# Second feed-forward products: 8 or 9 of 16 units by Strassen's scheme instead of 7, with one to three weight sums of a unit made in DRAM

## The chip, the cores and the metric

The kernel runs on one core of a Trainium2 chip. The metric is the device time of one execution in microseconds (us), lower is better. Before the change it is 1324.59 us, the median of 3 runs (1323.66 to 1324.63).

## What is computed

A trunk of four layers works on 256 tokens of width 1024 in float32. Each layer adds a token mixer and then a feed-forward block to the residual stream; the mixers are retention (layers 0 and 3), a convolution module (layer 1) and stick-breaking attention (layer 2). A last RMS norm follows. The change is in the feed-forward block:

```
def squared_relu_mlp(xn, w1, w2):          # w1: 1024 x 4096, w2: 4096 x 1024
    h = jax.nn.relu(xn @ w1)
    return (h * h) @ w2

for i in range(DEPTH):                     # DEPTH = 4
    x = x + mixer(rms_norm(x, norm_mix[i]))
    x = x + squared_relu_mlp(rms_norm(x, norm_ffn[i]), ffn_w1[i], ffn_w2[i])
```

## The kernel before

**Numbers.** Every float32 operand of a large product is split into a rounded part (`hi`, type fp32r) and the rest (`lo`); a product is three matmuls, hi·hi, hi·lo and lo·hi (`triple`, L721, one 128x512 matmul each). For a weight, ACT copies `hi` (L367) and DVE subtracts to get `lo` (L374).

**Weights.** All weights are packed on the host into 220 chunks of 128 x 2048 floats (1 MB), in the order in which they are used. One chunk holds two units of 1024 columns. SP loads chunks with plain DMAs (L349) into three buffers `raw`; the units' hi and lo lie in five buffers each (`wh`, `wl`). SP issues its DMAs strictly in its own order, and so do POOL, DVE, ACT and PE with their instructions: an instruction that waits for a semaphore holds back all that stand behind it on its engine. A scheduler orders the instructions of each engine; in the stick-breaking mixer PE and ACT keep the order in which the code was written.

**Second feed-forward product** (`down`). The 4096 inner columns are 16 units `kb` of 256. The result has four 128x512 blocks C[t, c] (two token halves t, two column halves c) in PSUM. A plain unit is eight block products, 24 matmuls. A unit of the list `FAST` uses Strassen's scheme in Winograd's form: seven block products, 21 matmuls. With A the unit's 2 x 2 activation blocks and B its weight blocks, the seven products take A11, A12, A22 and the sums S1 = A21 - A22, S2 = A11 - S1, S3 = A11 - A21, S4 = A12 - S2 on one side, and B11, B21, B22 and T1 = B11 + B12, T2 = T1 + B22, T3 = B12 + B22, T4 = T2 + B21 on the other (`fast_unit`). T1, T2 and T4 are added by DVE (L415, L417, L419). T3 is made in a temporary by two transfers: SP loads B12 (L385), then POOL issues a transfer that accumulates B22 onto it (L386); the tile is fetched two fast units ahead (`sum_ahead`). The S sums are made by DVE in the stage before, as each inner column group comes out of the first product (L680 to L682), and are split at L684 (ACT) and L685 (DVE). Before the change seven of 16 units are fast in each layer; 13 units (`MIXED`) come first, fast and plain in turn, and three plain ones (`REST`) last.

**POOL elsewhere.** POOL also adds squares for the norms (L519, and L527 in `norm_r`), adds halves of the retention's q and k squares (L968), writes the convolution's strips, and in stick-breaking attention clears one tile for each of the four head groups b (L1637). ACT then writes a masked copy of q into this tile (L1640), and PE reads it (L1662) together with the image of k that ACT makes next (L1633).

Of the kernel before, what the change touches and what calls it, by code (L numbers as in the profile page):

```python
# [15 lines left out]
P = 128  # L16
# [42 lines left out]
FAST = (5, 6, 9, 12, 13, 14, 15)  # L59
MIXED = (0, 1, 5, 2, 6, 3, 9, 12, 4, 13, 14, 7, 15)  # L60
REST = (8, 10, 11)
# [7 lines left out]
def _plan():  # L69
    u = []  # L70
    for i in range(DEPTH):
# [30 lines left out]
        u += [("ffn_w2", i, "a", kb, c * 512) for kb in MIXED for c in range(2)]  # L102
        u += [("ffn_w2", i, "a", kb, c * 512) for c in range(2) for kb in REST]
# [6 lines left out]
NCHUNK = NUNIT // UPC  # L110
DECAY = [PLAN.index(u) // UPC + n for u in (PLAN[DST * UPC], ("ret_w_in", 1, "b", 0, DK)) for n in range(RH)]


def _pack_weights(inp):
    out = np.empty((NCHUNK, P, UPC * 1024), np.float32)
    for n, (name, l, kind, kb, c0) in enumerate(PLAN):
# [3 lines left out]
        if kind == "qk":  # L120
            blk = np.concatenate([blk[:, c0 : c0 + 256], blk[:, D + c0 : D + c0 + 256]], axis=1)
        else:
            blk = blk[:, c0 : c0 + nc_]
        o = out[n // UPC, :, (n % UPC) * 1024 : (n % UPC + 1) * 1024]
# [119 lines left out]
class Trunk:  # L244
    def __init__(self, ctx, tc, xT, w, prm, cst, fin, gn, out):
# [18 lines left out]
        self.sums, self.later = [], []  # L264
# [72 lines left out]
    def unit_hi(self, key):  # L337
# [3 lines left out]
        if o == 0:  # L341
# [3 lines left out]
            else:  # L345
                self.rawt = self.raw.tile([P, RAWW], F32, name=self.nm("raw"), tag="raw")
                h = 1024 if n < 4 else UPC * 1024
                for a in range(0, UPC * 1024, h):
                    nc.sync.dma_start(self.rawt[:, a : a + h], self.w_d[n][:, a : a + h])  # L349
# [27 lines left out]

    def sum_ahead(self, l):
        nc = self.nc
        m = len(self.ahead)  # L380
        if m < len(FAST):
            kb = [k for k in MIXED if k in FAST][m]
            d = self.w_d[PLAN.index(("ffn_w2", l, "a", kb, 0)) // UPC]
            t = self.tmp()
            nc.sync.dma_start(t, d[:, 1024:1536])  # L385
            self.tc.keep_in_program_order(nc.gpsimd.dma_start(t, d[:, 1536:2048], accum_op=ALU.add))  # L386
            self.ahead[kb] = t


    def fast_unit(self, name, l, kb):  # L390
# [13 lines left out]
        with self.tc.issue_after(self.lo_ins):  # L404
            hi, lo = self.unit((name, l, "a", kb, 0))
        out = [(hi[:, c : c + 512], lo[:, c : c + 512]) for c in (0, 512)]
        o = self.un % UPC * 1024
        assert PLAN[self.un] == (name, l, "a", kb, 512) and o
        self.un += 1
        b11, b21, t1, b22 = (self.rawt[:, i * 512 : (i + 1) * 512] for i in range(4))  # L410
        t3 = self.ahead[kb]
        self.sum_ahead(l)
        t2, t4 = (self.tmp() for _ in range(2))
        with self.tc.issue_after(self.lo_ins):
            nc.vector.tensor_add(t1, b11, t1)  # L415
        parts(self.rawt[:, 1024:2048])
        nc.vector.tensor_add(t2, t1, b22)  # L417
# [3 lines left out]
        out[2], out[3] = out[3], out[2]  # L421
        return out
# [99 lines left out]
    def norm_r(self, halves=True):  # L522
        nc = self.nc
        sq, n = self.sq, 2
        if halves:
            sq, n = sq[:, :S], 1
            nc.gpsimd.tensor_add(sq, sq, self.sq[:, S:])  # L527
# [122 lines left out]
    def ffn(self, i, nxt):  # L650
        nc = self.nc
        last = nxt is None
        h, rb, fast, room = [], [], {}, []

        def spare(n):
            if n < 4:
                return self.bigt(F32R)
            if n < 6:
                if n == 4:
                    room.append(self.cp.tile([P, RH * 384], F32R, name=self.nm("room"), tag="decay"))  # L660
                return room[0][:, (n - 4) * 512 : (n - 3) * 512]
            return self.zp.tile([P, 512], F32R, name=self.nm("z"), tag=f"z{n - 6}")

        def act(ps):
# [9 lines left out]
            p = len(h) // 2  # L674
            how = "dve" if p < 4 else "act"
            h.extend((self.split(s[:, :S], how), self.split(s[:, S:], how)))
            if p in FAST:
                x = self.tmp()
                s3, s1, s2, s4 = (x[:, n * P : (n + 1) * P] for n in range(4))
                nc.vector.tensor_sub(v3(x[:, :S], 2, P), v3(s[:, :S], 2, P), v3(s, 2, S)[:, :, P:])  # L680
# [1115 lines left out]
```

## Time and profile before

| | us |
|---|---|
| median of 3 runs | 1324.59 |
| the profiled execution | 1323.18 |
| its span, first to last instruction | 1321.4 |
| PE busy in the span | 1311.8 (99%) |
| DVE busy | 1090.9 (83%) |
| ACT busy | 869.7 (66%) |
| POOL busy | 185.3 (14%) |

The profile is of one execution, 1.4 us shorter than the median; 1.8 us of it lie outside the span. The four second feed-forward products stand at 293 to 377, 567 to 651, 858 to 942 and 1231 to 1315 us of the span, stick-breaking attention at about 651 to 757, the second retention at about 942 to 1125. A matmul's busy time overlaps the next one's, so the distance between starts, not the mean of one, tells PE's pace.

### The profile page before, as it was taken

The numbers are of one execution on the slowest core, as the hardware profiler recorded it, in microseconds if no ns is written. First come the engines' busy times: TensorE is split into PE (matmuls) and PEld (weight loads), VectorE is DVE, ScalarE is ACT, GpSimd is POOL, SyncE is SP. The second block draws the span as 40 slices with busy tenths as digits, with TensorE's granted clock in tenths as the row PEclk, the third lists the DMA queues.
The fourth block names the chain that finished last, engine by engine and source line by source line (L and its number), as shares of the span: only waits on it lengthen the run. The fifth ranks groups of instructions, "written<-read, shape, count | busy, mean of one in ns | idle before, by whom it ended". The sixth has DMA issues, their size and how long they took to land.

```text
span 1321.4 us, 20394 instructions
## 1 busy us (share of the span) xinstructions
PE 1311.8 (99%) x7679; PEld 1129.8 (86%) x7679; DVE 1090.9 (83%) x1845; ACT 869.7 (66%) x1419; POOL 185.3 (14%) x197
## 2 busy tenths in 40 slices
PE   9999999999999999999999999999999999999998
PEld 8988888888899898888888898888888888888886
DVE  7988877888988688789878588889898776799896
ACT  7555546885666478866768678856665554567664
POOL 3654411001009120010000010010120000100100
PEclk9999999999999999999999999999999999999999
DMA  8566655558785645587443355586554554555773
GB/s 313 206 219 231 228 207 190 193 190 264 234 304 153 207 178 194 189 245 247 170 183 128 128 194 190 190 269 227 219 185 174 190 180 158 201 204 182 243 237 114
DMA packets 54690, 269.43 MB, mean 204 GB/s; under 512 B 6336, under 2 KB 11584, under 8 KB 27200
## 3 DMA queue, kind: packets, MB, share of 16 engines
q1 hardware_dynamic: 47968, 253.45, 54.4%
q0 software_dynamic: 5760, 12.06, 4.4%
q10 hardware_dynamic: 864, 2.62, 0.6%
q8 instruction: 60, 0.98, 0.3%
q14 instruction: 38, 0.31, 0.1%
HBM read 261.46 MB, written 6.65 MB: 203 GB/s over the span
## 4 chain that ended last, share of the span: by engine, by line
PE 97%; DVE 1%; ACT 1%; POOL 0%; issue 0%; POOLq 0%; ACTq 0%
PE acc L604 22%; PE acc L721 19%; PE acc L600 11%; PE acc L1145 6%; PE acc L1147 6%; PE acc L1146 6%; PE mis L721 6%; PE acc L584 3%; PE acc L585 3%; PE acc L586 3%; PE mis L604 2%; PE acc L1313 1%; PE mis L600 1%; PE acc L1446 1%; PE mis L464 1%; PE mis L1034 1%
## 5 line engine op out<-in xcount | busy, mean ns | idle before, releaser
L374 DVE TENSOR_TENSOR wl<-raw,wh 128x1024 fp32r<-128x1024 f32 (+1 forms) x412 | 505.0, 1236 | 110.3 <-ACT wh L367 107.4
L367 ACT CAST wh<-raw 128x1024 fp32r<-128x1024 f32 (+1 forms) x412 | 423.9, 1041 | 198.3 <-PE acc L1147 67.2
L604 PE MATMUL acc<-z,wh 128*128 128x512 f32 x1152 | 399.4, 393 | 0.0
L600 PE MATMUL acc<-z,wl 128*128 128x256 f32 x1152 | 317.6, 280 | 0.0
L604 PEld LDWEIGHTS acc<-z,wh 128*128 128x128 f32 x1152 | 214.2, 187 | 47.1
L721 PE MATMUL acc<-wh,big 128*128 128x512 f32 x704 | 228.7, 391 | 0.0
L600 PEld LDWEIGHTS acc<-z,wl 128*128 128x128 f32 x1152 | 216.9, 189 | 2.4 <-DVE t L629 0.3
L721 PEld LDWEIGHTS acc<-wh,big 128*128 128x128 f32 x704 | 132.2, 188 | 27.1
L1145 PE MATMUL acc<-wh,z 128*128 128x512 f32 x352 | 138.6, 394 | 0.0
L1147 PE MATMUL acc<-wh,z 128*128 128x512 f32 x352 | 137.3, 390 | 0.0
L1146 PE MATMUL acc<-wl,z 128*128 128x512 f32 x352 | 137.2, 390 | 0.0
L721 PE MATMUL acc<-wl,big 128*128 128x512 f32 x352 | 137.0, 389 | 0.0
L386 POOL DMA_DIRECT2D t<-in_w x28 | 24.9, 1089 | 458.5 <-DMA t<-in_w 327.5
L628 ACT COPY t<-acc 128x256 f32<-128x256 f32 x154 | 53.2, 372 | 47.1 <-PE acc L604 45.5
L1145 PEld LDWEIGHTS acc<-wh,z 128*128 128x128 f32 x352 | 66.1, 188 | 15.2 <-issue 2.2
L1147 PEld LDWEIGHTS acc<-wh,z 128*128 128x128 f32 x352 | 66.1, 188 | 14.9 <-issue 0.8
L721 PEld LDWEIGHTS acc<-wl,big 128*128 128x128 f32 x352 | 66.1, 188 | 13.4
L1146 PEld LDWEIGHTS acc<-wl,z 128*128 128x128 f32 x352 | 66.1, 188 | 13.3
L519 POOL TENSOR_TENSOR t<-t,t 128x512 f32<-128x512 f32 x15 | 24.2, 1613 | 340.8 <-ACT t L514 310.5
L629 DVE TENSOR_TENSOR t<-acc,t 128x256 f32<-128x256 f32 x154 | 59.5, 419 | 13.6 <-ACT t L628 12.6
L399 ACT CAST wh<-raw 128x1024 fp32r<-128x1024 f32 x28 | 29.5, 1052 | 58.5 <-DVE raw L415 56.2
L584 PE MATMUL acc<-z,wh 128*128 128x256 f32 x224 | 63.7, 284 | 0.0
(312 smaller groups left out, 2314.3 us busy)
## 6 DMA issues: line engine op xcount, KB each, us to landing
raw<-in_w SPq DMA_DIRECT2D x214, 1024.0 KB, 4.9
t<-in_w SPq DMA_DIRECT2D x28, 256.0 KB, 5.5
t<-in_w POOLq DMA_DIRECT2D x28, 256.0 KB, 6.0
strip<-st POOLq DMA_DIRECT2D x36, 128.0 KB, 3.8
big<-strip SPq DMA_DIRECT2D x18, 256.0 KB, 5.9
big<-in_gn SPq DMA_DIRECT2D x16, 256.0 KB, 5.3
raw<-in_w SPq DMA_DIRECT2D x7, 512.0 KB, 7.8
raw<-hd SPq DMA_DIRECT2D x8, 263.0 KB, 5.5
```

What stands on the lines that cost most here:

```text
L367: nc.scalar.copy(hi[:, s], src[:, s])
L374: self.lo_ins = self.nc.vector.tensor_sub(lo[:, s], src[:, s], hi[:, s]).ins
L584: nc.tensor.matmul(o, wh[:, kk, cs], ah, start=st, stop=False, **kw)
L585: nc.tensor.matmul(o, wh[:, kk, cs], al, start=False, stop=False, **kw)
L600: mm = nc.tensor.matmul(ps[m][:, :S], wl[:, kk, cs], a[:, :S], start=first and kk == 0, stop=False, **kw)
L604: nc.tensor.matmul(ps[m], wh[:, kk, cs], a, start=False, stop=last and kk == 3, **kw)
L628: nc.scalar.copy(o[:, s], ps[m][:, S:])
L629: nc.vector.tensor_add(o[:, s], ps[m][:, :S], o[:, s])
L721: mm = nc.tensor.matmul(o, l, r, start=start and n == 0, stop=stop and n == 2, skip_group_check=True)
L1145: nc.tensor.matmul(ps[t], zh[:, s], wh[:, kk], start=k == 0, stop=False, skip_group_check=True)
L1146: nc.tensor.matmul(ps[t], zh[:, s], wl[:, kk], start=False, stop=False, skip_group_check=True)
L1147: nc.tensor.matmul(ps[t], zl[:, s], wh[:, kk], start=False, stop=k == 7, skip_group_check=True)
```

## The change

Layers 0 and 1 get eight fast units and layers 2 and 3 nine, so 34 instead of 28. The packed order of a fast unit becomes B21, B11, B22, B12. A new table `AHEAD` names, for each layer, chunks of earlier stages and a number m from 1 to 3: when that chunk is loaded, `make_sums` makes the first m of T1, T3 and T2 for one fast unit in a DRAM tile. SP copies B12 into it once or twice, POOL issues an accumulating transfer of B11 (and B22) onto that, and for m = 3 POOL copies T1 and accumulates B22 onto the copy. Layer 0 has seven such units with m = 2, layer 1 six with m = 1, layers 2 and 3 nine with m = 3. When the fast unit itself is loaded, SP takes 1536 columns from the weights, T1 from the DRAM tile in place of B12, and T3 and T2 into temporaries. What was not made ahead is made as before. On the activation side S1 is written over A21 and split with the rest of the activations, so three sums of 128 columns are split apart and not four. `norm_r` in the second retention adds on DVE and no longer on POOL.

```diff
-FAST = (5, 6, 9, 12, 13, 14, 15)
-MIXED = (0, 1, 5, 2, 6, 3, 9, 12, 4, 13, 14, 7, 15)
-REST = (8, 10, 11)
+FAST = 2 * [(3, 5, 7, 9, 12, 13, 14, 15)] + 2 * [(3, 5, 7, 9, 11, 12, 13, 14, 15)]
+MIXED = 2 * [(0, 1, 3, 5, 2, 7, 9, 4, 12, 13, 6, 14, 15)] + 2 * [(0, 1, 3, 5, 2, 7, 9, 11, 4, 12, 13, 14, 15)]
+REST = 2 * [(8, 10, 11)] + 2 * [(6, 8, 10)]
+AHEAD = {
...
+    2: [(n, 3) for n in (110, 112, 114, 116, 118, 121, 129, 133, 137)],
+    3: [(n, 3) for n in (163, 166, 169, 172, 175, 178, 181, 184, 196)],
+}
...
+                made = self.made.get((key[1], key[3])) if key[2] == "f" else None
+                if made:
+                    h = 1536
+                for a in range(0, UPC * 1024 // h * h, h):
                     nc.sync.dma_start(self.rawt[:, a : a + h], self.w_d[n][:, a : a + h])
+                if made:
+                    d, m = made
+                    nc.sync.dma_start(self.rawt[:, h : h + 512], d[:, :512])
+                    self.fetched = [self.tmp() for _ in range(m - 1)]
+                    for a, t in enumerate(self.fetched):
+                        nc.sync.dma_start(t, d[:, 512 * (a + 1) : 512 * (a + 2)])
...
+            if self.un // UPC in JOBS:
+                self.make_sums(*JOBS[self.un // UPC])
...
+    def make_sums(self, l, kb, m):
+        nc = self.nc
+        w = self.w_d[CHUNK[l, kb]]
+        d = self.dram.tile([P, m * 512], F32, name=self.nm("sums"), tag=f"sums{l}_{kb}", bufs=1)
+        n = min(m, 2)
+        src = w[:, 1536:2048].unsqueeze(1).to_broadcast([P, n, 512])
+        self.tc.keep_in_program_order(nc.sync.dma_start(v3(d[:, : n * 512], n, 512), src))
+        nc.gpsimd.dma_start(d[:, : n * 512], w[:, 512 : 512 + n * 512], accum_op=ALU.add)
+        if m == 3:
+            nc.gpsimd.dma_start(d[:, 1024:], d[:, :512])
+            nc.gpsimd.dma_start(d[:, 1024:], w[:, 1024:1536], accum_op=ALU.add)
+        self.made[l, kb] = d, m
...
-            nc.gpsimd.tensor_add(sq, sq, self.sq[:, S:])
+            (nc.vector if halves == "dve" else nc.gpsimd).tensor_add(sq, sq, self.sq[:, S:])
...
+                s3, s2, s4 = (x[:, n * P : (n + 1) * P] for n in range(3))
+                nc.vector.tensor_sub(s3, a11, a21)
+                nc.vector.tensor_sub(a21, a21, a22)
+                nc.vector.tensor_sub(s2, a11, a21)
+                nc.vector.tensor_sub(s4, a12, s2)
...
-                    self.norm_r()
+                    self.norm_r("dve" if j else True)
```

Three places show how the instructions move. Line numbers after the change are higher (L1637 becomes L1697, L374 becomes L395, L400 becomes L432, L419 becomes L459).

POOL before, from the end of layer 1's second product on: the last two accumulating transfers, the four cleared tiles of stick-breaking attention, the next norm's first add.

```order
L386 DMA t_1371_6840<-in_w 128x512
L386 DMA t_1388_6923<-in_w 128x512
L1637 MEMSET big_7500 128x512
L1637 MEMSET big_7675 128x512
L1637 MEMSET big_7856 128x512
L1637 MEMSET big_8031 128x512
L519 TENSOR_TENSOR t_1749_8448<-t_1745_8413,t_1748_8446 128x512
```

POOL after, inside stick-breaking attention: `sums` are the DRAM tiles of the jobs at chunks 112, 114, 116 and 118; DMAHW is the landing of a transfer that SP issued, DMASW of one that POOL issued.

```order
L408 DMA sums_7542<-sums_7542 128x512 [waits DMASW7_49,DMASW5_49]
L1697 MEMSET big_7604 128x512 [waits PE_49]
L408 DMA sums_7688<-sums_7688 128x512 [waits DMASW6_49,DMASW0_49]
L409 DMA sums_7542<-in_w 128x512 [waits DMASW7_49,DMASW1_49]
L409 DMA sums_7688<-in_w 128x512 [waits DMASW0_49]
L406 DMA sums_7868<-in_w 128x1024 [waits DMAHW4_49]
L408 DMA sums_7868<-sums_7868 128x512 [waits DMASW4_49,DMASW3_49]
L1697 MEMSET big_7784 128x512 [waits PE_49]
L409 DMA sums_7868<-in_w 128x512 [waits DMASW4_49]
L406 DMA sums_8060<-in_w 128x1024 [waits DMAHW7_49]
L408 DMA sums_8060<-sums_8060 128x512 [waits DMASW6_49]
L1697 MEMSET big_7970 128x512 [waits DVE_49]
```

The four tiles were cleared one after the other before; now the tiles of b = 0, 1 and 2 each stand behind an L406 and an L408 of a job, and these wait for landings.

DVE before, one fast unit of the last layer (kb 12): the first half's lo, T1, T2, T4, and the lo of the second half, T3, T2 and T4.

```order
L374 TENSOR_TENSOR wl_13554<-raw_13551,wh_13553 128x1024
L415 TENSOR_TENSOR raw_13551<-raw_13551 128x512
L417 TENSOR_TENSOR t_2858_13560<-raw_13551 128x512
L419 TENSOR_TENSOR t_2859_13561<-t_2858_13560,raw_13551 128x512
L400 TENSOR_TENSOR wl_13564<-raw_13551,wh_13563 128x1024
L400 TENSOR_TENSOR wl_13569<-t_2828_13425,wh_13568 128x512
L400 TENSOR_TENSOR wl_13569<-t_2858_13560,wh_13568 128x512
L400 TENSOR_TENSOR wl_13576<-t_2859_13561,wh_13575 128x512
```

DVE after, the fast unit kb 13 of the last layer (`raw_13941`) between parts of its neighbours.

```order
L459 TENSOR_TENSOR t_2984_14004<-t_2979_13993,raw_13989 128x512
L432 TENSOR_TENSOR wl_13917<-t_2960_13908,wh_13916 128x512
L395 TENSOR_TENSOR wl_13949<-raw_13941,wh_13948 128x1024
L432 TENSOR_TENSOR wl_13953<-raw_13941,wh_13952 128x1024
L459 TENSOR_TENSOR t_2996_14052<-t_2991_14041,raw_14037 128x512
L432 TENSOR_TENSOR wl_13958<-t_2966_13944,wh_13957 128x512
L432 TENSOR_TENSOR wl_13958<-t_2967_13945,wh_13957 128x512
L432 TENSOR_TENSOR wl_13965<-t_2972_13956,wh_13964 128x512
```

The adds of T1 and T2 are gone where m = 3, and the add of T4 (L459) now stands a unit or more ahead of its use.

POOL before, in the second retention's first head: the halves of q's squares, the add of `norm_r`, and the halves of k's and of the next heads'.

```order
L968 TENSOR_TENSOR big_10329<-t_2147_10324 128x256
L527 TENSOR_TENSOR t_2146_10322<-t_2146_10322 128x256
L968 TENSOR_TENSOR big_10329<-t_2167_10406 128x256
L968 TENSOR_TENSOR big_10475<-t_2181_10470 128x256
L968 TENSOR_TENSOR big_10475<-t_2195_10534 128x256
```

DVE after, at the same place: `norm_r`'s add is L566.

```order
L558 TENSOR_TENSOR t_2208_10507<-t_2206_10503,t_2207_10505 128x512
L395 TENSOR_TENSOR wl_10679<-raw_10671,wh_10678 128x1024
L1036 TENSOR_TENSOR t_2218_10535<-t_2210_10511,cst 128x512
L1037 TENSOR_TENSOR t_2219_10536<-t_2210_10511,cst 128x512
L566 TENSOR_TENSOR t_2208_10507<-t_2208_10507 128x256
```

The add left POOL's queue for DVE's, three instructions behind the sum that it reads.

More of the change, by code (lines that the diff above doesn't have):

```diff
@@ L263, in __init__ @@
         self.rest = self.end = None
-        self.sums, self.later = [], []
+        self.sums, self.later, self.made = [], [], {}
         nc = self.nc
@@ L375, in unit_lo @@
         return hi, lo
+    def make_sums(self, l, kb, m):
[10 more added lines that the diff above has]
+        self.made[l, kb] = d, m
     def sum_ahead(self, l):
         nc = self.nc
[L380 to L387, printed above, removed]
+        kbs = [kb for kb in FAST[l] if kb not in self.ahead and self.made.get((l, kb), (0, 0))[1] < 2]
+        if kbs:
+            w, t = self.w_d[CHUNK[l, kbs[0]]], self.tmp()
+            nc.sync.dma_start(t, w[:, 1536:2048])
+            self.tc.keep_in_program_order(nc.gpsimd.dma_start(t, w[:, 1024:1536], accum_op=ALU.add))
+            self.ahead[kbs[0]] = t
     def fast_unit(self, name, l, kb):
@@ L420, in fast_unit @@
         parts(t4)
-        out[2], out[3] = out[3], out[2]
-        return out
+        return [out[i] for i in (1, 0, 2, 3, 4, 5, 6)]
     def unit_raw(self, key, tag, eng=None):
@@ L732, in down @@
         C = {}
+        quick, mixed, late_kb = FAST[i], MIXED[i], REST[i]
         self.ahead = {}
```

115 lines of the change are left out of this document (71 added, 44 removed).

## The prediction

> **What bounds the kernel now.** I began with the page's busy times and its chain of waits, then asked who PE waited for, and then for the four stages of the second product.
>
> ```profile
> span 1321.4 us, 20394 instructions
> PE 1311.8 (99%) x7679; PEld 1129.8 (86%) x7679; DVE 1090.9 (83%) x1845; ACT 869.7 (66%) x1419; POOL 185.3 (14%) x197
> ...
> PE 97%; DVE 1%; ACT 1%; POOL 0%; issue 0%; POOLq 0%; ACTq 0%
> ```
>
> PE is busy for 99% of the span, and the chain that ends last lies on it for 97%. Nothing else bounds the whole. Its waits for others are few:
>
> ```profile
> PE mis L301 <- POOL t L273: 1.3, 1, 1.3
> PE mis L464 <- POOL t L527: 0.7, 1, 0.7
> ```
>
> So the time falls only where PE has fewer columns to stream, or where one of these waits goes; it rises wherever PE is made to wait. The stage that the change shortens, seen alone (only the matmuls of L721; columns: stretch, its length, PE busy and count, granted clock, DMA share, GB/s):
>
> ```profile
> 293.00:377.00 84.00, 82.78 (x363) 1.00 0.83 273
> 567.00:651.00 84.00, 82.76 (x363) 1.00 0.76 244
> 858.00:942.00 84.00, 82.75 (x363) 1.00 0.76 249
> 1231.00:1315.00 84.00, 82.81 (x363) 1.00 0.63 201
> ```
>
> The four stages take the same time for the same 363 matmuls, 82.75 / 363 = 0.228 us each, at full clock: PE never starves there, whatever DMA and DVE do.
>
> **Part by part.**
>
> *Fewer matmuls.* A unit that becomes fast drops one block product, three matmuls. Six more units are fast (34 against 28): 18 x 0.228 = 4.1 us less. The built order has 18 PE rows fewer, so this part does happen. It counts in full only if the operands still come in time.
>
> *DVE and ACT in the second product.* The rows of DVE by shape in the third of these stages (count | busy, mean ns | idle before):
>
> ```profile
> L374 DVE TENSOR_TENSOR wl<-raw,wh 128x1024 fp32r<-128x1024 f32 x24 | 28.8, 1222 | 3.1 <-ACT wh L367 2.7
> L400 DVE TENSOR_TENSOR wl<-t,wh 128x512 fp32r<-128x512 f32 x21 | 13.3, 686 | 3.2 <-ACT wh L399 3.2
> L419 DVE TENSOR_TENSOR t<-t,raw 128x512 f32<-128x512 f32 x7 | 4.9, 693 | 0.2
> L417 DVE TENSOR_TENSOR t<-raw 128x512 f32<-128x512 f32 x7 | 4.8, 692 | 0.2
> L415 DVE TENSOR_TENSOR raw<-raw 128x512 f32<-128x512 f32 x7 | 4.8, 686 | 0.0
> ```
>
> A fast unit costs DVE two lo's of 1024 columns, three of 512 and three adds: 2 x 1.22 + 6 x 0.69 = 6.6 us, against 21 x 0.228 = 4.8 us on PE. A plain unit costs DVE 2.4 and PE 24 x 0.228 = 5.5 us. With m = 3 two adds go: 5.2 us. Over layer 2 or 3 that is 14 adds less (9.7 us) and two more units at 5.2 - 2.4 = 2.8 us: DVE ends 4 us lighter, although four fast units in a row leave it 4 x 0.4 = 1.6 us behind, which the plain unit before them (3.1 us to spare) covers. Layers 0 and 1 keep two or three adds and take one more unit, which comes out within 1 us of before, with at most two fast units in a row. I cost it at nothing; without that cover it would be some 1 us a stage. On ACT a fast unit keeps its 3584 columns of hi. The sums S cost DVE four small subtractions instead of three and a lo of 384 columns instead of 512, in the first product, where they lie beside matmuls: nothing.
>
> *Transfers in the second product.* T3's accumulation goes for 27 of 34 units (layer 1 keeps all eight, layer 0 one); 768 KB of weights and one to three loads of 256 KB come instead. For m = 3 the unit moves 1.5 MB, as before (1 MB, 256 KB and an accumulation of 256 KB). SP's loads of T3 and T2 wait for a temporary, and the next chunk stands behind them. In the stage above ACT already waited for T3's accumulation without PE noticing:
>
> ```profile
> L399 ACT CAST wh<-t 128x512 fp32r<-128x512 f32 x21 | 11.7, 617 | 5.6 <-DMA t<-in_w 4.4 <-PE acc L721 1.2
> ```
>
> So 4 us late in a stage stays hidden, and I cost this at nothing.
>
> *The wait that goes.* PE's 0.7 us at L464 ends with POOL's add of `norm_r`:
>
> ```profile
> 959.95 0.38 PE L464 MATMUL mis<-cst,t 128*128 128x1 f32 x2 [0.68 <-POOL t L527]
> ...
> 953.77 4.81 POOL L968 TENSOR_TENSOR big<-t 128x256 f32<-128x256 f32 x1 [56.81 <-ACT t L959]
> 958.54 1.35 POOL L527 TENSOR_TENSOR t<-t 128x256 f32<-128x256 f32 x1
> ...
> 953.81 0.69 DVE L519 TENSOR_TENSOR t<-t,t 128x512 f32<-128x512 f32 x1
> ```
>
> What it reads is ready on DVE at 953.81 + 0.69 = 954.5, but POOL is held by the add before it. On DVE the add comes after one lo and two products (1.22 + 2 x 0.69 us), about 957, and PE asks at 959.95 - 0.68 = 959.3: the 0.7 us goes, and nothing is late next. At worst it stays.
>
> *The jobs: transfers into DRAM.* Each adds one SP issue behind a chunk's load and one to three POOL instructions. The loads queued behind it come a little later, which ACT's casts don't feel, since they wait for PE to free their buffers and not for DMA:
>
> ```profile
> L367 ACT CAST wh<-raw 128x1024 fp32r<-128x1024 f32 (+1 forms) x412 | 423.9, 1041 | 198.3 <-PE acc L1147 67.2
> ```
>
> What PE can feel is POOL's queue. In stick-breaking attention the clearing of ACT's tile now waits behind an accumulation's landing (the order above). ACT keeps its written order there, so its masked copy of q holds everything behind it: k's image, the casts, the exponentials; PE waits for k's image. The price, from the loads of chunks 116 (for b = 1), 117 and 118 (for b = 2):
>
> ```profile
> 680.55 0.33 SPq L349 DMA_DIRECT2D raw<-in_w  x1
> ...
> 688.63 0.33 SPq L349 DMA_DIRECT2D raw<-in_w  x1
> ...
> 696.37 0.33 SPq L349 DMA_DIRECT2D raw<-in_w  x1
> ...
> 691.49 0.94 ACT L1640 ACTIVATE big<-mis,prm 64x256 f32<-64x256 f32 x2
> 692.45 0.69 ACT L1633 ACTIVATE big<-mis,prm 128x512 f32<-128x512 f32 x1
> ...
> 694.32 1.06 PE L1662 MATMUL mis<-big,big 128*128 128x128 f32 x8
> ...
> 707.78 0.94 ACT L1640 ACTIVATE big<-mis,prm 64x256 f32<-64x256 f32 x2
> 708.75 0.69 ACT L1633 ACTIVATE big<-mis,prm 128x512 f32<-128x512 f32 x1
> ...
> 711.28 0.94 PE L1662 MATMUL mis<-big,big 128*128 128x128 f32 x7
> ```
>
> For b = 1 ACT needs the tile 691.49 - 680.55 = 10.9 us after the load's issue, and PE has 694.32 - 693.14 = 1.2 us to spare: due 12.1 us after the issue. For b = 2: 11.4 + 1.8 = 13.2 us. What has to fit in: SP's copy of 512 KB behind the load, POOL's accumulation of 512 KB, POOL's next issue, and the clearing.
>
> ```profile
> raw<-in_w SPq DMA_DIRECT2D x214, 1024.0 KB, 4.9
> t<-in_w SPq DMA_DIRECT2D x28, 256.0 KB, 5.5
> ...
> raw<-in_w SPq DMA_DIRECT2D x7, 512.0 KB, 7.8
> ...
> q1 hardware_dynamic: 47968, 253.45, 54.4%
> q0 software_dynamic: 5760, 12.06, 4.4%
> ...
> L386 POOL DMA_DIRECT2D t<-in_w x28: 872/888/1702, 299.6 to 1270.1; - x28
> ...
> DMA to landing us min/median/max: 4.0/6.0/11.4
> ...
> 864.51 3.60 POOL L386 DMA_DIRECT2D t<-in_w  x4 [88.95 <-DMA t<-in_w]
> ...
> L1637 POOL MEMSET big<- 128x512 f32 x2 | 1.1, 526 | 44.8 <-DVE big L768 30.8 <-PE acc L721 14.0
> ```
>
> No row has a transfer from DRAM to DRAM. The nearest for the copy is the 256 KB behind a load, 5.5 us; another 256 KB on SP's queue is 0.544 x 1321.4 / 253.45 x 0.262 = 0.7 us: 6.2, at most the 7.8 of 512 KB in a crowd. The nearest for the accumulation is L386, 256 KB: 4.0 alone, 6.0 median, 11.4 at most; another 256 KB on POOL's queue is 0.044 x 1321.4 / 12.06 x 0.262 = 1.3 us: 5.3 alone. The chain is 0.4 + 6.2 + Y + 0.9 + 0.5 = 8.0 + Y, Y the accumulation's landing. Alone (5.3) it takes 13.3: PE waits 1.2 us at b = 1 and 0.1 at b = 2. At 6.0 it takes 14.0: 1.9 + 0.8 = 2.7 us. I take Y = 5.5, so 1.4 + 0.3 = 1.7 us in all: near the lone value, since each of the four stages issues its first four at once, 16 of the 28 in the median, but above it, since the next chunk's load falls on top. Below zero it can't go. The Trainium skill, page "DMA: Bandwidth & Descriptors", section "Anatomy of one DMA — SWDGE (gpsimd) path", prices such a transfer at 2.0 us plus its bytes at 436 GB/s; that would be an estimate of 3.2 us for 512 KB, and the sum would be without any wait. The trace disagrees for accumulations: half the bytes never landed in less than 4.0 us.
>
> In the second retention the last heads' adds stand behind the jobs of chunks 163 and 166, and PE wants the squares that they make:
>
> ```profile
> 979.27 0.33 SPq L349 DMA_DIRECT2D raw<-in_w  x1
> ...
> 1000.78 1.06 PE L985 MATMUL mis<-big,cst 128*32 128x512 f32 x8
> ```
>
> The first row is the load of chunk 166. The chain of 13.5 us after it and two adds of 1.35 (L527's row) end at 995.5: nothing, unless Y passes 10.
>
> **The sum.** -4.1 - 0.7 + 1.7 = -3.1 us. The profiled execution (1323.2) becomes 1320.1; on the median, 1.4 us above it, 1324.6 becomes 1321.5. About 0.2%, 2.65 us, is what a measurement of this kernel can tell from no change.
>
> **The rivals.**
>
> *No wait at all* (18%): the accumulation lands within 4.1 us and the tile is cleared in time; or POOL's queue is quicker than I read it. Then -4.8: 1319.8. Against it stand the 4.0 least for half the bytes and the copy's place behind the load. This is the case of that page's price.
>
> *The loads crowd the accumulation* (30%): the next chunk is loaded 8 us after the job's (688.63 against 680.55), about when the accumulation begins, at 680.55 + 0.4 + 6.2 = 687.2. With Y = 6.0 + 1.3 = 7.3 the chain is 15.3: 3.2 + 2.1 = 5.3 us, and the time stays within 0.2%: +0.5, 1325.1. For it speaks the median; against it, the lone 4.0, and that here one load meets the accumulation, not four accumulations and a load.
>
> *Slower: POOL's queue starves ACT* (16%). Same place, stick-breaking attention, but accumulations into DRAM at the long end. From Y = 8.4 on, 2 x 8.0 + 2 x 8.4 - 12.1 - 13.2 = 7.5 us are lost and the change loses over 0.2%; at the 11.4 of the row it is 13.5 us, 1333. For it: 11.4 was seen, and jobs overlap there. Against it: those came four at once. The same section of that page says that a transfer's end waits for the write's receipt, which takes longest into HBM; no run here shows an accumulation into DRAM.
>
> *The covers fail* (4%): DVE or SP late in the second products, 1 us a stage: again about no change.
>
> **How the numbers follow.** The likeliest case (32%) is the sum, 1321.5; for waits of 0.5 to 2.1 us it reaches from 1320.3 to 1321.9. Faster: 32 + 18 = 50%; same: 30 + 4 = 34%; slower: 16%. The range takes in no wait (1319.8, less 0.4 of scatter) and the crowded case up to 6.8 us of wait, 1326.6; the long end beyond is left out.
>
> **What would show it.** Right: L721 with 360, 360, 357 and 357 matmuls at 0.228 us; no L464 wait in the second retention; ACT idle before the masked copies of b = 1 and b = 2 with POOL's clearing as releaser, and PE idle of 1 to 2 us behind it. Wrong: PE gaps in the second products, at the retention's squares, or in the first products where the jobs run; ACT waits there of 4 us and more; or PE matmuls that no longer start 0.228 us apart.

## The result, and the profile after

| | us |
|---|---|
| before, median of 4 runs | 1324.61 (1323.66 to 1324.69) |
| after, median of 4 runs | 1358.47 (1355.10 to 1360.51) |
| ratio | 1.0255, 95% interval 1.0231 to 1.0279 |
| profiled execution after | 1355.1, its span 1353.3 |

The change makes the kernel 34 us slower; the forecast was 3.1 us faster. The profiled execution is the quickest of the four, so what follows accounts for 31.9 us of span. One execution of the experiment with POOL held took 4653 us where the other three took 1348.8 to 1350.1, and it is left out of that ratio.

The page of the changed kernel: span, busy times, the chain that ended last.

```profile
span 1353.3 us, 20691 instructions
...
PE 1315.5 (97%) x7661; PEld 1129.2 (83%) x7661; DVE 1087.0 (80%) x1899; ACT 883.8 (65%) x1451; POOL 215.0 (16%) x244
...
PE 85%; DMA 6%; DVE 4%; issue 2%; ACT 1%; POOL 1%; SPq 0%; DVEq 0%; POOLq 0%; ACTq 0%
```

PE has 18 matmuls fewer and is busy 3.7 us longer (1315.5 against 1311.8), but the span is 31.9 us longer: PE waits. The chain that was PE for 97% now runs through DMA, DVE and POOL for 11%. Whom PE waits for (in total, times, longest):

```profile
PE mis L1714 <- ACT big L1700: 12.8, 3, 7.4
PE acc L780 <- DVE acc L830: 3.7, 2, 1.8
PE mis L1391 <- issue: 2.9, 2, 2.1
PE mis L1161 <- DVE t L1158: 2.6, 1, 2.6
PE mis L1045 <- POOL big L1028: 1.9, 1, 1.9
PE mis L883 <- ACT t L870: 1.4, 1, 1.4
PE mis L311 <- POOL t L283: 1.3, 1, 1.3
```

Of these only the last was there before. The wait at L464 (now L503) is gone. To see where each wait counts, I cut both traces at the starts of the first and the last matmul of each second product (L721, now L780):

| stage (us) | before | after | difference |
|---|---|---|---|
| layer 0 up to its second product | 293.4 | 294.6 | +1.2 |
| second product, layer 0 | 83.6 | 86.7 | +3.1 |
| layer 1 up to its second product | 190.4 | 193.8 | +3.3 |
| second product, layer 1 | 83.6 | 85.0 | +1.4 |
| layer 2 up to its second product (stick-breaking) | 207.4 | 228.4 | +21.0 |
| second product, layer 2 | 83.6 | 82.2 | -1.4 |
| layer 3 up to its second product (retention) | 289.5 | 294.0 | +4.5 |
| second product, layer 3 | 83.1 | 81.7 | -1.4 |
| end | 6.9 | 7.0 | +0.1 |

Two thirds of the loss is in stick-breaking attention. The matmuls of L780 alone, in the four second products (columns as in the prediction, with the weight loads behind PE):

```profile
294.50:382.00 87.50, 82.75 (x360) 67.30 (x360) 1.00 0.74 261
574.90:661.00 86.10, 82.73 (x360) 67.30 (x360) 1.00 0.85 256
888.00:972.00 84.00, 81.74 (x357) 66.81 (x357) 1.00 0.74 261
1264.00:1347.00 83.00, 81.46 (x357) 66.89 (x357) 1.00 0.62 216
```

The counts are those forecast, and layers 2 and 3 gain the 1.4 us (6 x 0.228) that were forecast. Layers 0 and 1 have the fewer matmuls too and lose them again to waits.

**Stick-breaking attention, b = 1.** SP's chunk load and the job's copy; POOL's accumulation, the copy of T1 and the clearing of ACT's tile; then ACT. One fence for each engine's timeline (start, length, instruction, idle time before it and its releaser).

```profile
695.63 0.33 SPq L362 DMA_DIRECT2D raw<-in_w  x1
696.01 0.56 SPq L405 DMA_DIRECT2D sums<-in_w  x1
```

```profile
707.91 0.81 POOL L406 DMA_DIRECT2D sums<-in_w  x1 [2.43 <-DMA sums<-in_w]
715.01 0.55 POOL L408 DMA_DIRECT2D sums<-sums  x1 [6.29 <-DMA sums<-in_w]
715.54 0.55 POOL L1697 MEMSET big<- 128x512 f32 x1
```

```profile
706.38 0.68 ACT L1693 ACTIVATE big<-mis,prm 128x512 f32<-128x512 f32 x1
716.13 0.95 ACT L1700 ACTIVATE big<-mis,prm 64x256 f32<-64x256 f32 x2 [9.06 <-POOL big L1697]
```

The copy lets POOL go 11.9 us after its issue (696.01 to 707.91), the accumulation holds it for 7.1 more (707.91 to 715.01), and the clearing ends 20.5 us after the load's issue (716.1 against 695.6). It was due after 12.1. ACT stands idle for 9.1 us and PE for 7.4.

What follows the wait is not told by the waits. The 8 us behind the waits at b = 0, 1 and 2 (stretch, length, busy time and count of PE, weight loads, DVE, ACT and POOL, then granted clock, DMA share, GB/s):

```profile
691.70:699.70 8.00, 7.53 (x32) 5.66 (x33) 6.43 (x19) 7.85 (x12) 1.40 (x2) 0.79 0.72 206
717.10:725.10 8.00, 7.84 (x33) 6.22 (x34) 6.45 (x19) 7.33 (x12) 0.81 (x1) 0.73 0.58 133
739.00:747.00 8.00, 7.63 (x40) 6.07 (x41) 5.98 (x17) 7.85 (x13) 1.33 (x2) 1.00 0.60 147
```

Behind the first two, the granted clock is 0.79 and 0.73: 8 x 0.21 + 8 x 0.27 = 3.8 us more. The three waits (12.8 us) and the clock make 16.6 of the stage's 21.0 us. Four smaller groups of waits in it, for DVE and ACT, add 2.7 us; 1.7 us are not accounted for.

**Second product of layer 0.** DVE, where PE waits for L830, the update of a result block, before the plain units `REST` go on with it:

```profile
360.81 2.35 DVE L395 TENSOR_TENSOR wl<-raw,wh 128x1024 fp32r<-128x1024 f32 x2
363.08 0.69 DVE L826 TENSOR_TENSOR big<-big,big 128x512 f32<-128x512 f32 x1
...
369.48 0.70 DVE L856 TENSOR_TENSOR acc<-acc,big 128x512 f32<-128x512 f32 x1
370.08 0.70 DVE L830 TENSOR_TENSOR acc<-acc,big 128x512 f32<-128x512 f32 x1
```

DVE has no idle time here: it comes out of two fast units in a row (14 and 15, the last with all sums made by DVE), and has the combination of the products still to do, between the lo's of the plain units. PE's wait ends at 370.8 us. In layer 0 a second one of 1.4 us follows at 378.1, for ACT's L870, which scales a finished result block; the chain of waits runs from L830 to it. Layer 1 has the first wait alone, 1.8 us.

**Second retention.** POOL ahead of PE's squares L1045, and SP ahead of the gate's weights. First SP's load of chunk 166 and its job's copy, then POOL:

```profile
1007.03 0.33 SPq L362 DMA_DIRECT2D raw<-in_w  x1
1007.40 0.56 SPq L405 DMA_DIRECT2D sums<-in_w  x1
```

```profile
1019.39 0.81 POOL L406 DMA_DIRECT2D sums<-in_w  x1 [6.03 <-DMA sums<-in_w]
1027.63 0.56 POOL L408 DMA_DIRECT2D sums<-sums  x1 [7.43 <-DMA sums<-in_w]
1028.19 1.83 POOL L1028 TENSOR_TENSOR big<-t 128x256 f32<-128x256 f32 x2
```

```profile
1126.04 0.57 SPq L405 DMA_DIRECT2D sums<-in_w  x1
1126.66 1.13 SPq L1145 DMA_DIRECT2D big<-in_gn  x2
```

```profile
1136.54 1.41 DVE L1154 SCALAR_TENSOR_TENSOR t<-mis,G,big 128x512 f32<-128x512 f32 x2 [5.80 <-DMA big<-in_gn]
```

The squares' adds stand behind the landing of chunk 166's accumulation, as the forecast had it. The copy took 12.0 us (1007.40 to 1019.39), the accumulation 8.2, and the adds end 23.0 us after the load's issue; 13.5 and two adds of 1.35 had been forecast. The gate's weights were loaded right behind a job's copy in SP's queue and came 5.8 us late for DVE.

### The profile page after: what moved, and what is told of

Same layout as the page of the kernel before. It is cut to its first block, busy times and chain, and to the rows that moved or that the text cites. A ratio compares the mean times of both kernels' runs of the same rounds, so it can differ in the third digit from the quotient of the medians.

```text
span 1353.3 us, 20691 instructions
## 1 busy us (share of the span) xinstructions
PE 1315.5 (97%) x7661; PEld 1129.2 (83%) x7661; DVE 1087.0 (80%) x1899; ACT 883.8 (65%) x1451; POOL 215.0 (16%) x244
## 3 DMA queue, kind: packets, MB, share of 16 engines
q0 software_dynamic: 11520, 31.20, 12.3%
## 4 chain that ended last, share of the span: by engine, by line
PE 85%; DMA 6%; DVE 4%; issue 2%; ACT 1%; POOL 1%; SPq 0%; DVEq 0%; POOLq 0%; ACTq 0%
PE acc L643 21%; PE acc L780 15%; PE acc L639 11%; PE mis L780 6%; PE acc L1205 4%; PE acc L1207 4%; PE acc L1206 4%; DMA sums<-in_w 3%; PE acc L623 3%; PE acc L624 3%; PE acc L625 3%; PE mis L643 2%; DVE wl L395 2%; DMA big<-in_gn 1%; PE acc L1506 1%
## 5 line engine op out<-in xcount | busy, mean ns | idle before, releaser
L395 DVE TENSOR_TENSOR wl<-raw,wh 128x1024 fp32r<-128x1024 f32 (+1 forms) x406 | 496.0, 1233 | 101.8 <-ACT wh L388 100.3
L388 ACT CAST wh<-raw 128x1024 fp32r<-128x1024 f32 (+1 forms) x406 | 418.7, 1041 | 203.7 <-PE acc L1207 60.3
L780 PE MATMUL acc<-wh,big 128*128 128x512 f32 x632 | 209.1, 391 | 3.7 <-DVE acc L830 3.7
L780 PEld LDWEIGHTS acc<-wh,big 128*128 128x128 f32 x632 | 118.7, 188 | 28.8 <-DVE acc L830 4.5
L780 PE MATMUL acc<-wl,big 128*128 128x512 f32 x316 | 123.0, 389 | 0.0
L431 ACT CAST wh<-t 128x512 fp32r<-128x512 f32 x102 | 60.3, 619 | 37.7 <-PE acc L780 12.2
L432 DVE TENSOR_TENSOR wl<-t,wh 128x512 fp32r<-128x512 f32 x102 | 66.1, 687 | 6.0 <-ACT wh L431 6.0
L780 PEld LDWEIGHTS acc<-wl,big 128*128 128x128 f32 x316 | 59.4, 188 | 11.9
L406 POOL DMA_DIRECT2D sums<-in_w x31 | 26.0, 873 | 264.5 <-DMA sums<-in_w 264.5
```

The source lines that it names most:

```text
L388: nc.scalar.copy(hi[:, s], src[:, s])
L395: self.lo_ins = self.nc.vector.tensor_sub(lo[:, s], src[:, s], hi[:, s]).ins
L431: nc.scalar.copy(h[:, c], t)
L432: self.lo_ins = nc.vector.tensor_sub(g[:, c], t, h[:, c]).ins
L780: mm = nc.tensor.matmul(o, l, r, start=start and n == 0, stop=stop and n == 2, skip_group_check=True)
```

## The experiments

Theory A: the jobs cost, mainly by POOL's queue. Theory B: more fast units starve PE. Theories and rivals C to H are defined in the expectations, where they come up. Each ratio is against runs of the kernel before on the same chip, whose median was 1322.2 to 1323.5 us.

**No sums made ahead.**

```diff
-AHEAD = { ... }
+AHEAD = {}
```

> No sum is made ahead (the table AHEAD is empty); the 34 fast units, their order and norm_r on DVE stay. Theory A (the loss comes from the jobs: POOL's queue holds back the clearing of ACT's tile, each wait is followed by matmuls at a lower granted clock, and the retention's squares and one load come late too): the stick-breaking stage comes back to 106 us and the 4.5 us of layer 3 go, what stays is -4.8 for matmuls and L503 and the waits of 4.0 and 2.2 us in the second products of layers 0 and 1; with T2, T3 and T4 all on DVE and up to four fast units in a row another 2 to 4 us each in layers 2 and 3: 1324 to 1332 us. Theory B (more fast units starve PE, whoever makes the sums): above 1340 us. Theory C (the forecast's covers are right and only the jobs cost): 1319.8 us.

Measured: 1351.59 us, ratio 1.0216 (1.0202 to 1.0230). The stick-breaking and retention stages are as before (207.0 and 288.4 us), and the second products take 89.6, 89.5, 93.4 and 87.1 us. PE's waits:

```profile
PE acc L775 <- DVE wl L427: 7.5, 10, 0.9
PE acc L775 <- DVE acc L825: 7.0, 4, 2.2
PE mis L775 <- ACT wh L426: 5.0, 3, 2.3
```

The time is theory B's, above 1340, and A's 1324 to 1332 was missed, but both theories hold for a part. The jobs are what costs in these two mixers, and with all sums on DVE the four second products together take 26 us more than before. So the forecast's cover in the second product fails: 7.0 us here is the wait for the combination (L825 is the line that was L830).

**The clearing on DVE.**

```diff
-                nc.gpsimd.memset(f, 0.0)
+                nc.vector.memset(f, 0.0)
```

> The changed kernel with one line different: the tile of each head group in stick-breaking attention is cleared by DVE and no longer by POOL; all jobs stay. Theory A (POOL's queue): the waits of ACT's masked copy for the clearing (18.5 us in three) go, and with them PE's waits of 3.2, 7.8 and 2.8 us and the slower matmuls behind them; the stage from the end of layer 1's second product to layer 2's loses 18 to 21 us: 1337 to 1341 us. Rival D (the jobs' traffic crowds the chunk loads, and ACT's casts would be late without the clearing too): no more than 8 us less, 1350 us or above. Rival E (the granted clock falls because of traffic or of more work in all, not because of waits): the windows behind b=0 and b=1 still show 0.73 to 0.79.

Measured: 1333.52 us, ratio 1.0072 (1.0056 to 1.0089): 25 us less than the changed kernel (by the ratios 1.83% or 24 us). POOL still waits for landings in this stage (an answer on the waits of 651 to 765 us):

```profile
POOL sums L406 <- DMA sums<-in_w: 65.8, 4, 35.4
```

but PE waits for nobody, and the clock stays full:

```profile
670.00:690.00 20.00, 20.00 (x101) 16.54 (x100) 14.80 (x47) 11.07 (x17) 2.17 (x3) 1.00 0.94 275
690.00:710.00 20.00, 20.00 (x102) 16.36 (x101) 18.13 (x35) 17.43 (x29) 3.61 (x5) 1.00 0.97 261
```

The stage is 207.0 us, 21.4 less. One instruction's place in POOL's queue was the 21 us. The time is below A's 1337 to 1341: in this execution the retention stage took 289.4 us against 294.0 in the changed kernel, though nothing there differs. D and E fall for this stage: the DMA engines were 0.94 to 0.97 busy and PE missed nothing.

**POOL held without any transfer**, in the kernel before:

```diff
-                nc.gpsimd.memset(f, 0.0)
+                n = (12, 32, 24, 0)[b]
+                if n:
+                    nc.gpsimd.tensor_copy(f, G["sc", b, 0])
+                for _ in range(n + 1):
+                    nc.gpsimd.memset(f, 0.0)
```

> The kernel before, with no transfer added: in stick-breaking attention POOL copies q and k into the tile of b = 0, 1 and 2 and clears it 13, 33 and 25 times in a row in place of once, so that the clearing ends about as late as in the changed kernel (estimated ACT waits 5, 9 and 5 us). Theory A (the wait for POOL alone is the loss, traffic isn't needed): PE waits 10 to 14 us behind ACT's masked copies, the granted clock falls to 0.7 to 0.8 for some 8 us behind the long waits, and the stage grows by 1.3 to 1.5 times PE's waits: 1336 to 1344 us. Rival D (it takes the jobs' traffic for the slow matmuls): the clock stays at 1.0 and the stage grows by no more than PE's waits.

Measured: 1349.64 us, ratio 1.0197 (1.0183 to 1.0212). The stage grows by 25.9 us, PE's waits behind ACT are 16.1:

```profile
PE mis L1658 <- ACT big L1644: 16.1, 3, 8.9
```

```profile
683.70:691.70 8.00, 7.77 (x28) 5.89 (x29) 6.46 (x19) 7.55 (x12) 1.40 (x3) 0.60 0.38 129
...
734.80:742.80 8.00, 7.80 (x28) 5.90 (x29) 5.69 (x17) 7.80 (x14) 0.00 (x0) 0.59 0.26 88
```

Theory A again: waits alone do it, with no transfer added (the DMA engines were busy 0.38 and 0.26 in these windows), and the clock goes down behind each of them. A microsecond of such a wait costs 25.9 / 16.1 = 1.6; the waits came out longer than I had meant, and with them the time (1336 to 1344 had been expected).

**Layer 2's jobs in its first product.**

```diff
-    2: [(n, 3) for n in (110, 112, 114, 116, 118, 121, 129, 133, 137)],
+    2: [(n, 3) for n in (124, 126, 127, 129, 130, 132, 133, 135, 137)],
```

> The changed kernel with the nine jobs of layer 2 moved: none in stick-breaking attention, all nine in layer 2's first feed-forward product (chunks 124 to 137). Theory A: the clearing waits for nothing, so the same 18 to 21 us go as with the clearing on DVE; nine jobs of three POOL transfers each in the 100 us of the first product have no reader near, so nothing comes back: 1337 to 1341 us. Rival D (a job's traffic costs wherever it runs): the first product of layer 2 gets longer by 5 us or more, and the time stays above 1345 us.

Measured: 1345.13 us, ratio 1.0165 (1.0149 to 1.0182). The stage is 216.1 us: 12.3 less than in the changed kernel, but 8.7 more than before. Waits in the first product, 770 to 875 us:

```profile
DVE wl L395 <- ACT wh L388: 23.7, 17, 5.2
ACT wh L388 <- DMA raw<-in_w: 21.1, 7, 5.8
...
PE acc L639 <- DVE t L668: 5.3, 2, 2.9
```

Here rival D is right. ACT's casts wait for chunk loads, 21.1 us in all, DVE waits for ACT, and PE for DVE. PE's two waits are 5.3 us, and in the 8 us behind each of them the granted clock was 0.79 and 0.81, an estimated 3.2 us more: together about the 8.7.

**The same with copies only.** In layer 2 POOL's three transfers of a job are left out:

```diff
-        n = min(m, 2)
+        n = m if l == 2 else min(m, 2)
...
-        nc.gpsimd.dma_start(d[:, : n * 512], w[:, 512 : 512 + n * 512], accum_op=ALU.add)
-        if m == 3:
+        if l != 2:
+            nc.gpsimd.dma_start(d[:, : n * 512], w[:, 512 : 512 + n * 512], accum_op=ALU.add)
+        if m == 3 and l != 2:
```

> The run with layer 2's nine jobs in its first product, with POOL's three transfers of each of these jobs left out (SP's copy fills all three parts of the DRAM tile instead, so the sums of layer 2 are not made). The stage from layer 1's second product to layer 2's was 216.1 us with the jobs there and 207.4 before. If the accumulations crowd the chunk loads (what POOL's queue moves), it comes back to 207 to 209 us. If it is SP's copy, in the same queue as the loads and just ahead of the next one, it stays at 213 us or more.

Measured: 1334.09 us, ratio 1.0091 (1.0064 to 1.0118). The stage is 207.1 us, and in the first product ACT waits only once for a load, 0.6 us:

```profile
ACT wh L388 <- PE acc L644: 5.2, 9, 2.3
...
ACT wh L388 <- DMA raw<-in_w: 0.6, 1, 0.6
```

So it is what POOL's queue moves that makes chunk loads late, not SP's copies, though these write more bytes here than in the run above (768 KB a job against 512). Which part of POOL's transfers does it is not shown: two accumulations and a copy of T1 went together, and with them half of the 1.5 MB that a job writes.

**norm_r on DVE alone**, in the kernel before:

```diff
-                    self.norm_r()
+                    self.norm_r("dve" if j else True)
```

> The kernel before with one edit of the change alone: the add of norm_r in the second retention on DVE. Theory A: PE's 0.7 us wait at L464 goes and nothing takes its place: 0.7 us less, 1323.9 us. Rival: DVE's two adds and the lo ahead of it make it as late: 1324.6 us, no change.

Measured: 1323.28 us, ratio 1.0004 (0.9995 to 1.0013): nothing in the time. The stage up to the last second product is 288.9 us against 289.5, so the 0.6 to 0.7 us are gone where they were looked for, but the interval of the time, 2.4 us wide, neither shows them nor quite rules them out. The profiled execution is the slowest of the eleven, since its convolution stage took 194.3 us against 190.4, with its work unchanged: PE waited 2.4 us at L1331, and the granted clock over the next 8 us was 0.79. The changed kernel has the same there (L1391, 2.1 us, 0.79). So the +3.3 us of this stage in the table above need not be an effect of the change; over all runs with the same convolution it came out between 189.3 and 194.3.

**The lists of before** in the new code, no sums ahead:

```diff
+FAST = 4 * [(5, 6, 9, 12, 13, 14, 15)]
+MIXED = 4 * [(0, 1, 5, 2, 6, 3, 9, 12, 4, 13, 14, 7, 15)]
+REST = 4 * [(8, 10, 11)]
+AHEAD = {}
```

> The changed kernel with the fast units of before (seven, in the order of before, in all four layers) and no sum made ahead; the new order of a unit's columns, the new S sums and norm_r on DVE stay. Theory F (more fast units in a row than DVE can feed cost the 4 to 10 us of each second product that were seen without the sums): the second products come back to 83.6 us and the time to that of before, 1322 to 1324 us. Rival G (the new code of a fast unit, in which T1 is added first and the lo of the second half follows it, is what makes PE wait): second products above 85 us, 1330 us or more.

Measured: 1326.12 us, ratio 1.0031 (1.0020 to 1.0043). Second products of 85.3, 85.2, 85.1 and 83.1 us: most of the 26 us is the lists, but 1.6 us a stage in three layers stay, which F doesn't explain; the time lies between the two forecasts. These 1.6 us lie at the first fast units of the stage (300 to 312 us):

```profile
ACT wh L426 <- DMA t<-in_w: 7.4, 1, 7.4
```

ACT waited 4.8 us there before. The first T3 lands late; why is not settled.

**Spaced fast units** in layers 0 and 1, with the clearing on DVE:

```diff
-MIXED = 2 * [(0, 1, 3, 5, 2, 7, 9, 4, 12, 13, 6, 14, 15)] + ...
+MIXED = 2 * [(0, 3, 1, 5, 7, 2, 9, 12, 4, 13, 14, 6, 15)] + ...
```

> The changed kernel with the clearing on DVE, and in layers 0 and 1 the same eight fast units in another order: the last one has a plain unit ahead of it, and no three of four are fast in a row. Theory F: the waits for DVE of 2.2 and 1.8 us at the end of the second products of layers 0 and 1 go, 86.6 becomes 82.9 us in each: 7 us less than with the clearing on DVE alone, 1325 to 1328 us. Rival G: those waits stay, 1332 to 1335 us.

Measured: 1329.70 us, ratio 1.0050 (1.0038 to 1.0062). The second products of layers 0 and 1 take 82.9 and 83.4 us where they took 86.6 and 86.6: F. (Of layer 1's 3.2 us only about half is the wait. With the clearing on DVE the granted clock behind its wait of 1.8 us was 0.79, an estimated 1.7 us; in the changed kernel it was 1.00 there and the stage took 85.0. The order also moves the earlier fast units, not only the last one.) The time is 4 us less and not 7, between the two forecasts, since in this execution the jobs took more elsewhere: 210.0 us up to layer 2's second product (a chunk load came 5.1 us late for ACT) and 295.6 up to layer 3's. With the same jobs these stages were 207.0 and 289.5 with the clearing on DVE alone. How late the accumulations make others differs between executions.

**Layers 2 and 3 alone**: layers 0 and 1 with the lists of before and no jobs, clearing on DVE.

```diff
+FAST = 2 * [(5, 6, 9, 12, 13, 14, 15)] + 2 * [(3, 5, 7, 9, 11, 12, 13, 14, 15)]
...
-    0: [(n, 2) for n in (26, 27, 28, 38, 40, 42, 45)],
-    1: [(n, 1) for n in (81, 83, 85, 87, 89, 91)],
```

> The changed kernel with the clearing on DVE, and layers 0 and 1 with the seven fast units and the order of before and no jobs; layers 2 and 3 keep nine fast units and all their jobs. Theories A and F together: second products 83.6, 83.6, 82.3 and 81.7 to 83 us, no wait in stick-breaking attention: 2 to 2.7 us faster than before, 1319.5 to 1320.5 us. Rival D (the traffic of the jobs of layers 2 and 3 still makes loads late): no faster than before, 1322 to 1328 us.

Measured: 1331.15 us, ratio 1.0066 (1.0049 to 1.0084). Layers 2 and 3 save 2.7 us in their second products (82.2 and 81.7) and lose 4.0 and 2.2 us ahead of them; layers 0 and 1 take 85.1 and 85.0, as with the old lists. Rival D, and slower than it said: here nine jobs with m = 3 cost more than the matmuls that they allow. The 4.0 us begin with a chunk load that came 5.1 us late for ACT; PE waited 2.3 us behind it, and the granted clock of 0.79 in the next 8 us is an estimated 1.7 more.

**Eight spaced units in all layers, thin jobs.**

```diff
+FAST = 4 * [(3, 5, 7, 9, 12, 13, 14, 15)]
+MIXED = 4 * [(0, 3, 1, 5, 7, 2, 9, 12, 4, 13, 14, 6, 15)]
+REST = 4 * [(8, 10, 11)]
+AHEAD = {i: [(n, 2) for n in range(a, a + 14, 2)] for i, a in enumerate((33, 77, 125, 189))}
```

> A version meant to beat both: eight fast units in all four layers in the order with a plain unit ahead of the last one, and seven jobs with m = 2 in each first feed-forward product, every second chunk; no job in a mixer, so the clearing may stay on POOL. Theory F with thin jobs: second products 82.9 us each as in layer 0 of the spaced run, no wait elsewhere, 4 x 0.65 = 2.6 us faster than before: 1320 to 1321 us. Rival D (a job's traffic makes chunk loads late wherever it runs): the first products get 1 to 4 us longer each and the time is 1324 to 1335 us.

**The same, no sums ahead** (`AHEAD = {}`).

> The same order with eight fast units in all four layers and no sum made ahead. Theory F: DVE needs 8 x 6.6 + 5 x 2.4 = 64.8 us for the mixed part, PE 8 x 4.8 + 5 x 5.5 = 65.9 us; DVE just keeps up, and what stays are waits of 1 to 2 us a stage as with the old lists, so second products of 83 to 85 us and 1322 to 1328 us. Rival H (it is the number of fast units, not their order): near the 87 to 93 us a stage of the run without sums, 1340 us or more.

Measured: 1319.55 us with thin jobs, ratio 0.9970 (0.9959 to 0.9982), and 1319.31 us without any, ratio 0.9970 (0.9959 to 0.9982). Both beat both kernels, the kernel before by 0.3%. Theory F's forecast was close for the first (1320 to 1321) and too slow for the second (1322 to 1328). The matmuls of L775 in the run without jobs:

```profile
294.00:378.00 84.00, 82.46 (x360) 67.37 (x360) 1.00 0.86 279
...
1229.20:1312.70 83.50, 82.14 (x360) 67.44 (x360) 1.00 0.67 204
```

The stages are 82.9, 82.9, 82.9 and 82.4 us, each 0.7 (3 x 0.228) less than before: 2.7 us of the 4, and no wait in a second product is left. The wait at L464, 0.7 us, went too, in the last retention stage (287.9 us against 289.5); the rest is not traced to a cause. Rival H falls: eight units without any help lost 6 us in layer 0 in one order and nothing in the other. And the sums made ahead are worth nothing here: with and without them the time is the same. Nor do these jobs cost anything: seven accumulations of 512 KB in a first product left no load late in layer 2's.

**Nine spaced units**, thin jobs:

```diff
+FAST = 4 * [(3, 5, 7, 9, 11, 12, 13, 14, 15)]
+MIXED = 4 * [(0, 3, 5, 7, 1, 9, 11, 12, 2, 13, 14, 4, 15)]
+REST = 4 * [(6, 8, 10)]
+AHEAD = {i: [(a + n, 2) for n in (0, 2, 4, 5, 7, 9, 10, 12, 14)] for i, a in enumerate((32, 76, 124, 188))}
```

> The thin-jobs version with a ninth fast unit in every layer: nine fast units, only four plain ones between them (groups of three, three, two and one), nine jobs with m = 2 in each first feed-forward product. Theory F (DVE sets it): a group of three costs DVE 3 x 5.9 + 2.4 = 20.1 us with m = 2 against 3 x 4.8 + 5.5 = 19.9 us on PE, so it just keeps up: another 4 x 0.68 us less, 1316 to 1318 us. Rival: the groups of three and the denser jobs bring waits of 1 us a stage or more and eat it: 1319 to 1326 us.

Measured: 1322.49 us, ratio 1.0000 (0.9989 to 1.0011). Second products of 83.9, 83.8, 83.8 and 82.0 us with 357 matmuls. PE waits for lo's again:

```profile
PE acc L775 <- DVE wl L390: 1.3, 3, 0.4
```

The rival: with groups of three the ninth unit's gain is lost in three layers of four. The waits listed for PE cover only 1.3 us of it.

## Why the prediction was wrong, by its own steps

**What bounds the kernel**: right for before; PE at 99% meant that any wait shows in full.

**Fewer matmuls**, -4.1 us: right in count and pace, and paid out in layers 2 and 3 (-1.4 each). In layers 0 and 1 it was lost to waits.

**Transfers in the second product**, at nothing: right, no wait of PE's points at them. But the count was off: T3's accumulation goes for 25 of the 34 units, not 27 (layer 1 keeps eight and layer 0 one; L418 runs nine times).

**DVE and ACT in the second product**, "I cost it at nothing": wrong in layers 0 and 1, +4.5 us where -1.4 was forecast, and right in layers 2 and 3. The step compared sums over units (6.6 us of DVE against 4.8 of PE) and looked for a plain unit before the row of fast ones. It left out what comes behind the last one: the combination on DVE, which PE's next blocks need. In the order with a plain unit ahead of the last fast one (the spaced run) both waits went, and with them 3.7 and 3.2 us.

**The wait that goes**, -0.7: right; the stage shows it in the run with that edit alone, the time doesn't.

**The jobs in stick-breaking attention**, +1.7: this step failed, by size and not by mechanism. PE waited 12.8 us, and the stage grew by 21.0. Place and chain were right (L1700 behind L1697 behind the landing of L406), and the slower rival was this one. For b = 1 the chain was 20.5 us and not 13.5. The accumulation took 7.1 us until POOL went on (5.5 taken, 7.3 in the crowded rival); the larger miss is SP's copy, 11.9 us where 6.2 was taken and 7.8 called the most. The range of a transfer that no row showed was cut at a median of other transfers, and all of the uncertainty was put on Y. Then two terms were missing: b = 0, whose tile stands behind a job as well (a wait of 2.9 us), and the clock behind a wait (3.8 us). The price that the Trainium skill gives for such a transfer (page "DMA: Bandwidth & Descriptors", section "Anatomy of one DMA — SWDGE (gpsimd) path"), an estimate of 3.2 us for 512 KB as the prediction worked it out, is far from what the page of the profile shows for POOL's accumulations (KB each, median us to landing; the first row is SP's copies, for which the prediction had taken 6.2):

```profile
sums<-in_w SPq DMA_DIRECT2D x25, 512.0 KB, 8.6
sums<-in_w POOLq DMA_DIRECT2D x25, 512.0 KB, 8.0
```

**The second retention's squares**, "nothing, unless Y passes 10": wrong, a wait of 1.9 us. It was the job looked at, chunk 166's. Y was 8.2 and did not pass 10; the copy took 12.0 us, 5.8 more than assumed, and with it the 5.3 us that were to spare were gone. The threshold had been set on one transfer of two. (Four of the six traces with this job have this wait.)

**Loads queued behind the jobs**, "ACT's casts don't feel it": wrong. It went by ACT's waits before, which were mostly for PE (1.5 us for loads). In the changed kernel they are 8.9 us for loads, 2.7 the longest, which cost PE 0.7 us; with nine jobs in a row they are 21.1 us in one first product, and 0.6 with copies only. The gate's weights in the second retention, on DVE, came 5.8 us late and cost PE 2.6; they stood behind a job's copy, and no run tells the copy from the accumulations there.

**The chances.** The slower rival had 16%, with 1333 at its long end. It happened, together with two covers that failed (4%) and an effect that had no case. They were weighed as if only one could happen, though one cause, slow transfers of the jobs, drives most of them.

Open: why the first T3 lands later with the new column order, and what decides in which execution the jobs delay the loads of layers 2 and 3.

## What to carry to other kernels

An instruction that other engines need must not stand in a queue behind one that waits for a transfer's landing; moving four clearings of less than 1 us each to DVE was worth 21 us in their stage. When an extra saving on the bound engine loads a helper, write out the helper's backlog unit by unit up to the last thing that it owes, and space the heavy units before buying help: here eight units in a spaced order gave the whole gain, and the transfers meant to relieve DVE brought nothing. For an operation that the trace doesn't show, keep the far end open, and don't price late starts as the wait alone.

## What the runs showed of the hardware

**PE's clock falls behind a wait: each time from 2.9 us on, sometimes from 1.8.** Six waits of 2.9 to 8.9 us (two in the changed kernel, three with POOL held, one with layer 2's jobs in its first product) were each followed by 8 us at a granted clock of 0.59 to 0.79. Shorter waits went both ways. In the changed kernel the clock stayed at 1.00 behind 1.8 us (end of layer 1's second product), 2.4 (b = 2) and 2.6 (L1161), but was 0.79 behind 2.1 us in the convolution; with the clearing on DVE it was 0.79 behind the same 1.8 us. So no threshold in the length of a wait follows from these runs. Behind the wait at b = 0 of the changed kernel, 128x512 matmuls:

```profile
696.24 0.63 PE L1207 MATMUL acc<-wh,z 128*128 128x512 f32 x1
696.66 0.63 PE L1205 MATMUL acc<-wh,z 128*128 128x512 f32 x1
...
697.74 0.40 PE L1205 MATMUL acc<-wh,z 128*128 128x512 f32 x1
697.97 0.39 PE L1206 MATMUL acc<-wl,z 128*128 128x512 f32 x1
```

Starts are 0.42 us apart and then 0.23. The Trainium skill, page "TensorE: Matmul & The Clock Gate", section "Part 1: The HAM clock gate (the "warmup" mystery)", says that the array drops to half its clock after an idle window of about 3.4 us and needs as much sustained work to come back. The trace agrees in the pace, and a clock of 0.79 over 8 us is what 3.4 us at half the clock would give (an estimate). In the idle time it does not: waits of 1.8 to 2.9 us, shorter than that window, were followed by it too.

**Many transfers on POOL's queue slow plain loads.** With nine jobs of two accumulations and a copy each in one first product, chunk loads came up to 5.8 us late; with SP's copies of 768 KB in place of all that, 0.6 us once. Seven jobs of one accumulation each, spread over every second chunk, made no load late in the same product. Whether it is the accumulating or the amount is not shown.
